# A hybrid decoder layer: 64-row and 64-column products of two heads issued by turns in branches A and C

## The chip, the cores and the metric

The kernel runs on one core of one Trainium2 chip. The time is the device time of one execution in microseconds (us); the median of repeated runs is quoted. All inputs and weights lie in the chip's memory at the start, and all outputs must be written there. One execution was also taken by the hardware profiler, and its records are what this document reads.

## The reference

One inference step of one layer, for a prompt of 1024 tokens and a sample group of 8 x 8 tokens that use the same weights. The model width is 1024. The input projection feeds four token mixers of 256 channels each; their outputs are projected, gated and summed, and attention to a memory and a feed-forward network follow.

```
def _layer(x, ...):
    h = x @ lp['w_in']
    ya = _sb_prompt(q, k, v, bias)      # A: stick-breaking attention, 4 heads x 64
    yb = gb * conv_out                  # B: short gated convolution
    yc, ... = _rwkv7(h[..., OFF_C:OFF_D], ...)   # C: RWKV-7, 4 heads x 64
    yd, sgu_v = _sgu(h[..., OFF_D:], ...)        # D: chunked gating MLP
    gates = sigmoid(x @ w_gate + b_gate)
    x = _ln(ALPHA * x + sum_i(gates_i * (branch_i @ w_branch_i)) @ w_o)
    x = _ln(ALPHA * x + memory attention(x))
    x = _ln(ALPHA * x + (relu(x @ w_up) ** 2) @ w_down)
```

Branch A, for each head and query, sums value rows with weights that are made from the scores of all earlier keys (a sigmoid of the score times the product of the "not stopped" factors after it). Branch C keeps a 64 x 64 state per head:

```
    def step(S, inp):
        r_t, w_t, k_t, v_t, a_t, b_t = inp
        sa = jnp.einsum('nhij,nhj->nhi', S, a_t)
        S = S * w_t[:, :, None, :] + sa[..., None] * b_t[:, :, None, :] + v_t[..., None] * k_t[:, :, None, :]
        return S, jnp.einsum('nhij,nhj->nhi', S, r_t)
```

The prompt begins with a zero state; each of the 8 sample sequences begins with a state of its own, 4 heads each, and its final state is an output.

## The kernel before

All of it is one program on five engines. TensorE (PE) multiplies 128 x 128 weights with up to 512 columns into PSUM; VectorE (DVE), ScalarE (ACT) and GpSimd (POOL) work between PSUM and SBUF, and SyncE (SP) issues most DMAs. A product in plain fp32 leaves two records on PE, one per pass; `mm`, the big projections (L117, L129), is split by hand into high and low parts in a faster type.

In time, the program does branch C at about 105 to 517 us, D to 569, A to 900, then the gates and branch projections, the output projection, the memory attention and the feed-forward network. The branches consist of small products with waits between them. So that PE has work there, `self.fill(step)` at set places draws the next units of the big projections from a generator (`units`): a fixed number of them for each kind of step. Behind that, a scheduler sets the final order on each engine from the code's order and its own estimate of times; the order on each engine is then fixed.

**Branch A** (`branch_a`). A step is one query block `i` of 128 queries, one block `ob` of up to 512 keys, a pair of heads `pr` and a head `hh` of it. The scores `z` (L470) of both heads are multiplied one behind the other; `sb_chunk` (L339 to L354) makes the weights of one head with Exp and Ln on ACT and a running sum on DVE. `turn` transposes them (`wtp`, L497) and copies them to SBUF (`wT`); `values` (L444) then multiplies them with V for that head into its 64 rows of `yps`, up to four products in a row. `late` and `turned` are lists that delay `turn` by two heads and `values` by one more. The sample's own attention (`zp`, L513, and `ysp`, L553) runs between; it already takes two pairs of heads by turns.

**Branch C**, chunks of 256 prompt tokens, in the order 0, sample, 1, 2, 3. `c_blocks` makes for each block of 128 tokens and each pair of heads the transposes `tk` (L947), then for each head four products of 64 rows x 128 columns in the PSUM tile `gr` (L955), which DVE masks into `LM` and `lm` (L956, L957); `c_solve` inverts a triangular matrix: its blocks go to memory (`Ld`) and come back spread out (`Li`, a DMA issued by SP), DVE sets the diagonal of `Li` (a memset, L996), and 31 pairs of DVE operations follow (`tpr`, `Ti`, L1002, L1003). `c_uw` (L1037, L1040) multiplies with the inverse; `c_chain` carries the state S through four steps of 64 tokens per chunk, and in each step multiplies S by WT (L1063), adds on DVE, and updates the state with two products for each pair of heads, tok by tok (L1069) and tok by SA (L1073), each 64 rows to 128 x 128, of which only the two 64 x 64 blocks of the own head are used (L1076). The products of 64 x 64 at L1080 take two heads by turns.

**The sample** (`c_sample`), for each pair of heads: for each head, 8 products `sas` (state times WT, L1105) and 8 products `yss` (state times r, 8 columns, L1106) turn by turn; DVE adds into `SAs` (L1107); a fill; the product `ym` (L1109); then twice a spread tile `ex` by DVE (L1113, 64 x 512) and a product `snp` of 64 rows x 512 columns (L1115). At the pair's end DVE adds `snp` to the state, scales it (L1116, L1117), and adds `yss` and `ym` into Y (L1120).

Of the kernel before, what the change touches and what calls it, by code (L numbers as in the profile page):

```python
# [8 lines left out]
F32 = mybir.dt.float32  # L9
# [20 lines left out]
HR = (slice(0, 64), slice(64, 128))  # L30
# [19 lines left out]
class Kern:  # L50
# [306 lines left out]
    def branch_a(self, ca):  # L357
# [78 lines left out]
        def values(pr, i, ob, hh, w, wT):  # L436

            top = ob == i // 4
            if top and hh == 0:
# [5 lines left out]
            if ob == 0 and hh == 1:  # L445
# [7 lines left out]
        for pr in range(2):  # L453
            smp = self.sample_a(pr, own, bias, am, rows, wP)
            alone = False
            for i in range(8):
# [7 lines left out]
                for ob in range(i // 4, -1, -1):  # L464
# [6 lines left out]
                    for hh in range(2):  # L471
# [10 lines left out]
                        if turned:  # L482
                            values(*turned.pop(0))
# [4 lines left out]
        for a in turned:  # L488
            values(*a)
        for a in late:  # L490
            values(*turn(*a))
# [434 lines left out]
    def c_blocks(self, d):  # L926
# [16 lines left out]
        def products(pr, b):  # L943
# [5 lines left out]
            nc.scalar.copy(X[:nb, pb, :, 1, :], ps[:nb, 0:128].rearrange("p (h i) -> p h i", h=2))  # L949

            lm = cc.tile([128, 2, 2, 128], F32, name="lm", tag="lm", bufs=2)
            for hh in range(2):
                g = self.psw.tile([128, 4, 128], F32, name="gr", tag="gr", bufs=2)
                for j, (p, q) in enumerate(((bh, at), (bh, rt), (kh, at), (kh, rt))):
                    nc.tensor.matmul(g[:nb, j, :nb], p[HR[hh], pr, cs], q[HR[hh], pr, cs], start=True, stop=True)  # L955
                nc.vector.tensor_mul(LM[:nb, pb, hh, :, :nb], g[:nb, 0:2, :nb], lte)  # L956
                nc.vector.tensor_mul(lm[:nb, hh, :, :nb], g[:nb, 2:4, :nb], lte)  # L957
# [86 lines left out]
    def c_chain(self, d):  # L1044
# [3 lines left out]
        wide = lambda pr: slice(128 * pr, 128 * pr + 128)  # L1048
        tok, Mrb, WT, rt, Y, pc = (d[q] for q in ("tok", "Mrb", "WT", "rt", "Y", "pc"))
# [6 lines left out]
        for kx in range(4):  # L1056
# [4 lines left out]
            yps, sn = st[:, 0, 256:384], st[:, 1, 0:256]  # L1061
# [1231 lines left out]
```

## Time and profile before

| what | value |
|---|---|
| median of 3 runs (lowest to highest) | 2307.57 us (2305.55 to 2320.82) |
| the profiled execution's own time | 2307.98 us |
| its span in the trace | 2305.9 us |
| PE matmuls busy | 2213.4 us, 96% |
| weight loads (PEld), beside the matmuls | 1973.8 us, 86% |
| DVE, ACT, POOL busy | 1379.5, 973.6 and 424.9 us |
| chain of waits, PE's share | 74% |

The page sums the busy time of each engine and cuts the span into slices; the table of groups adds the instructions of one line; the timeline gives single instructions or runs of like ones (x8 means eight records from the first's start to the last's end). In the square brackets of a row stand the idle time of its engine before it and what ended that. The ends of matmuls are modelled and they overlap, so from one start to the next is less than a record's duration. PEclk is the granted TensorE clock as a share of full speed: 1.00 is 2.4 GHz, 0.50 is 1.2 GHz.

### The profile page before, as it was taken

What the parts mean: (1) busy time and instruction counts of PE and PEld (TensorE: products, weight loads), DVE (VectorE), ACT (ScalarE), POOL (GpSimd) and SP (SyncE); (2) the same over time, 40 slices, a digit from 0 to 9 for tenths busy, and PEclk for the clock granted to TensorE, in tenths of its full rate; (3) what the DMA queues carried; (4) which work ended last, traced back from release to release, by engine and by line L of the source; (5) the groups of instructions that cost most, each with busy time, mean ns of one, the idle gap of its engine ahead of it and who ended that gap; (6) DMA issues with size and microseconds to landing.
All of it is one profiled execution on the core that took longest, in us unless ns stands there. A gap on an engine that the chain in (4) does not pass through costs nothing.

```text
span 2305.9 us, 36127 instructions
## 1 busy us (share of the span) xinstructions
PE 2213.4 (96%) x13582; PEld 1973.8 (86%) x13582; DVE 1379.5 (60%) x2746; ACT 973.6 (42%) x1880; POOL 424.9 (18%) x484
## 2 busy tenths in 40 slices
PE   8998999999999999999999999999699999999997
PEld 8987687788889989998998878878699999788886
DVE  3357468645666576344333787668576777655548
ACT  4333153125554556444322466425334444543432
POOL 0111111112310310024120410000345454100100
PEclk9999799999999999999999999999899999999999
DMA  5322232135433434555323255633488677975535
GB/s 189 101 75 82 57 107 83 42 106 179 146 130 118 145 97 159 181 164 168 128 71 132 92 197 170 234 108 137 138 286 279 236 238 239 312 255 182 180 122 169
DMA packets 186070, 359.40 MB, mean 156 GB/s; under 512 B 36312, under 2 KB 92776, under 8 KB 185896
## 3 DMA queue, kind: packets, MB, share of 16 engines
q1 hardware_dynamic: 175448, 321.52, 42.7%
q0 software_dynamic: 10448, 35.57, 4.5%
q8 instruction: 107, 1.75, 0.3%
q14 instruction: 67, 0.55, 0.1%
HBM read 252.18 MB, written 104.84 MB: 155 GB/s over the span
## 4 chain that ended last, share of the span: by engine, by line
PE 74%; DMA 9%; DVE 9%; issue 3%; ACT 3%; POOL 1%; SPq 1%; DVEq 0%; ACTq 0%; POOLq 0%
PE mm L117 23%; PE m L117 13%; PE dn L1964 11%; PE mm L129 7%; PE sc L129 3%; PE pp L117 2%; PE yps L444 1%; PE ds L1969 1%; PE wtp L497 1%; PE gr L955 1%; DVE wlo L106 1%; DVE tpr L1002 1%; DMA Li<-Ld 1%; ACT whi L100 1%; DMA add<-gate 1%
## 5 line engine op out<-in xcount | busy, mean ns | idle before, releaser
L117 PE MATMUL mm<-ah,whi 128*128 128x384 f32 (+1 forms) x1176 | 397.1, 338 | 8.4 <-ACT ah L277 4.6
L117 PE MATMUL mm<-al,whi 128*128 128x384 f32 (+1 forms) x1176 | 393.5, 335 | 1.4 <-DVE al L278 1.4
L117 PE MATMUL mm<-ah,wlo 128*128 128x384 f32 (+1 forms) x1176 | 393.6, 335 | 1.1 <-DVE wlo L106 1.1
L1964 PE MATMUL dn<-dop 128*128 128x512 f32 x1344 | 318.8, 391 | 2.9 <-ACT dop L1661 2.7
L1964 PEld LDWEIGHTS dn<-dop 128*128 128x128 f32 x1344 | 251.7, 188 | 60.0 <-ACT dop L1661 4.5
L106 DVE TENSOR_TENSOR wlo<-wraw,whi 128x1024 fp32r<-128x1024 f32 (+2 forms) x177 | 196.2, 1118 | 162.7 <-ACT whi L100 162.3
L100 ACT CAST whi<-wraw 128x1024 fp32r<-128x1024 f32 (+1 forms) x162 | 166.0, 1032 | 257.6 <-PE mm L117 105.3
L117 PEld LDWEIGHTS mm<-ah,whi 128*128 128x128 f32 x1176 | 225.5, 192 | 20.0 <-issue 7.2
L117 PEld LDWEIGHTS mm<-al,whi 128*128 128x128 f32 x1176 | 225.2, 191 | 10.2 <-issue 6.5
L117 PEld LDWEIGHTS mm<-ah,wlo 128*128 128x128 f32 x1176 | 225.5, 192 | 7.0 <-issue 4.4
L1662 DVE TENSOR_TENSOR dop<-wraw,dop 128x512 fp32r<-128x512 f32 x224 | 151.7, 715 | 118.8 <-ACT dop L1661 118.5
L117 PE MATMUL m<-xht,wo 128*128 128x272 f32 x1024 | 202.4, 293 | 18.1 <-ACT wo L1661 10.5
L1661 ACT CAST dop<-wraw 128x512 fp32r<-128x512 f32 x224 | 131.2, 619 | 168.4 <-PE dn L1964 116.2
L117 PEld LDWEIGHTS m<-xht,wo 128*128 128x128 f32 x1024 | 165.5, 192 | 18.9 <-ACT wo L1661 10.7
L129 PE MATMUL mm<-wlo,ah 128*128 128x512 f32 (+1 forms) x488 | 169.1, 349 | 1.5 <-DVE wlo L106 1.4
L129 PE MATMUL mm<-whi,ah 128*128 128x512 f32 (+1 forms) x488 | 169.5, 349 | 0.7 <-ACT stD L636 0.5
L117 PE MATMUL m<-xh,wo 128*128 128x272 f32 x768 | 153.9, 294 | 6.3 <-DVE r L1876 6.3
L129 PE MATMUL mm<-whi,al 128*128 128x512 f32 (+1 forms) x448 | 155.8, 348 | 0.0
L117 PE MATMUL m<-xlt,wo 128*128 128x272 f32 x512 | 149.4, 292 | 0.0
L117 PEld LDWEIGHTS m<-xh,wo 128*128 128x128 f32 x768 | 124.8, 192 | 7.1 <-ACT wo L1661 2.6
L117 PE MATMUL m<-xl,wo 128*128 128x272 f32 x384 | 112.0, 292 | 0.0
L129 PEld LDWEIGHTS mm<-wlo,ah 128*128 128x128 f32 x488 | 92.9, 190 | 15.6 <-DVE wlo L106 2.5
(506 smaller groups left out, 4377.5 us busy)
## 6 DMA issues: line engine op xcount, KB each, us to landing
wraw<-hs SPq DMA_DIRECT2D x112, 256.0 KB, 3.4
wraw<-in_w_up SPq DMA_DIRECT2D x38, 512.0 KB, 4.4
wraw<-in_w_gate SPq DMA_DIRECT2D x32, 512.0 KB, 3.6
dw<-in_w_down SPq DMA_DIRECT2D x32, 512.0 KB, 5.1
hs<-sh SPq DMA_DIRECT2D x64, 256.0 KB, 2.6
wt<-dw SPq DMA_DIRECT2D x32, 512.0 KB, 5.6
wraw<-wt SPq DMA_DIRECT2D x64, 256.0 KB, 4.3
wraw<-in_w_down SPq DMA_DIRECT2D x48, 256.0 KB, 5.5
```

The costliest lines, as they stand in the source:

```text
L100: nc.scalar.copy(hi[:, c], raw[:, c])
L106: nc.vector.tensor_sub(lo[:, c], raw[:, c], hi[:, c].bitcast(F32))
L117: nc.tensor.matmul(ps[:, :n], a, b, start=first and i == 0, stop=last and i == len(steps) - 1, skip_group_check=not first)
L129: nc.tensor.matmul(ps[:, :n], a, b, start=i == 0, stop=i == len(steps) - 1)
L444: nc.tensor.matmul(y["ps"][HR[hh], 0:128], V[pr, ob][:, j, HR[hh]], wT[:, j, :], start=top and j == 0, stop=ob == 0 and j == w // 128 - 1)
L497: self.nc.tensor.transpose(ps[:b.shape[-1], j * 128:j * 128 + 128], b, self.ident)
L955: nc.tensor.matmul(g[:nb, j, :nb], p[HR[hh], pr, cs], q[HR[hh], pr, cs], start=True, stop=True)
L1002: nc.vector.tensor_mul(tv, Ti[:, 0:h, 0:t + 1], Li[:, 0:t + 1, t:t + 1].rearrange("p s o -> p o s").to_broadcast([128, h, t + 1]))
L1661: nc.scalar.copy(o[:, 0], src)
L1662: nc.vector.tensor_sub(o[:, 1], src, o[:, 0].bitcast(F32))
L1964: nc.tensor.matmul(ps[j], hs[:, a, c], w[:, b], start=first and k == 0, stop=last and k == 2, skip_group_check=n >= 16 and steps[n][0] in ...
L1969: nc.tensor.matmul(sp, rows[p][:, smp[i]].rearrange("p a n -> p (a n)"), ops[n][1][:, b], start=i != 2 and p == 0 and b == 0, stop=p == 15 ...
```

## The change

It sets the order of products in four places, and cuts work in two of them.

- **Branch A**: `values` takes both heads of a step. Their products alternate: head 0 into rows 0 to 63 of `yps`, head 1 into rows 64 to 127. `turned` is emptied when it holds two heads, so 24 runs of two heads replace 48 of one.
- **`c_blocks`**: both `gr` tiles are taken at once, and the four products of the two heads alternate.
- **`c_chain`**: the state's update computes only the own head's 64 x 64 block. Per step and term, four products of 64 x 64 replace two of 64 x 128; the alternating heads write different rows of PSUM.
- **`c_sample`**: `sas` of both heads alternate, then `yss` (now in a free part of the tile of `sas`). The two terms of the state's update are laid over one another in 128 rows: `tok` gets a copy in rows 64 to 127 (two more ACT copies per pair), `ex` is filled in both halves, and one product of 128 rows per head replaces two of 64. Three additions into Y replace two. The two fills of a pair stand together behind `yss`.

```diff
-        def values(pr, i, ob, hh, w, wT):
+        def values(*heads):
...
             for j in range(w // 128):
-                nc.tensor.matmul(y["ps"][HR[hh], 0:128], V[pr, ob][:, j, HR[hh]], wT[:, j, :], start=top and j == 0, stop=ob == 0 and j == w // 128 - 1)
+                for *_, hh, _, wT in heads:
+                    nc.tensor.matmul(y["ps"][HR[hh], 0:128], V[pr, ob][:, j, HR[hh]], wT[:, j, :], start=top and j == 0, stop=ob == 0 and j == w // 128 - 1)
...
-                        if turned:
-                            values(*turned.pop(0))
+                        if len(turned) == 2:
+                            values(*turned)
+                            turned.clear()
...
+            if smp:
+                nc.scalar.copy(tok[64:128, pb, 0, :], ps[0:64, 256:384])
+                nc.scalar.copy(tok[64:128, pb, 2, :], ps[0:64, 384:512])
...
+            g = [self.psw.tile([128, 4, 128], F32, name="gr", tag="gr", bufs=2) for _ in range(2)]
+            for j, (p, q) in enumerate(((bh, at), (bh, rt), (kh, at), (kh, rt))):
+                for hh in range(2):
+                    nc.tensor.matmul(g[hh][:nb, j, :nb], p[HR[hh], pr, cs], q[HR[hh], pr, cs], start=True, stop=True)
...
-            for pr in range(2):
-                nc.tensor.matmul(sn[:, wide(pr)], tok[q, 2 * pr + b, 1], tok[q, 2 * pr + b, 2], start=pr == 0, stop=False)
+            for pr, hh in own:
+                nc.tensor.matmul(sn[HR[hh], cols(pr)], tok[q, 2 * pr + b, 1, HR[hh]], tok[q, 2 * pr + b, 2, HR[hh]], start=pr == 0, stop=False)
...
-            for pr in range(2):
-                nc.tensor.matmul(sn[:, wide(pr)], tok[q, 2 * pr + b, 0], flat(SA[q, pr]), start=False, stop=pr == 1)
+            for pr, hh in own:
+                nc.tensor.matmul(sn[HR[hh], cols(pr)], tok[q, 2 * pr + b, 0, HR[hh]], SA[q, pr, hh, :], start=False, stop=pr == 1)
...
+            for hh, R in enumerate(HR):
+                spread(HR[1], tok[64:128, 2 * pr, 2, R], hh)
+            for s in range(8):
+                for hh, R in enumerate(HR):
+                    nc.tensor.matmul(st[0:64, hh, 0:64], wx[R, 64 * s:64 * s + 64], S0[R, s, :], start=s == 0, stop=s == 7, skip_group_check=True)
...
+            for s in range(8):
+                for hh, R in enumerate(HR):
+                    nc.tensor.matmul(st[R, hh, 64 + 8 * s:72 + 8 * s], S0[R, s, :], rt[R, pr, 8 * s:8 * s + 8], start=hh == 1 and s == 0, stop=s == 7, skip_group_check=True)
+            self.fill("smp")
+            self.fill("smp")
...
+            for hh, R in enumerate(HR):
+                spread(HR[0], SA[0:64, R], hh)
+            for hh, R in enumerate(HR):
+                nc.tensor.matmul(snp[R], tok[:, 2 * pr, 0, R], ex[hh], start=True, stop=True)
```

`spread` is the DVE multiplication that fills one half of an `ex` tile.

In branch A on PE (`yps<-wT,v` is a product of the weights of one head with V, and the number behind wT tells the heads apart), one head's run before:

```order
L444 MATMUL yps_5649<-wT_5652,v_5285 64x128 [waits DVE_49]
L444 MATMUL yps_5649<-wT_5652,v_5285 64x128
L497 MATMUL wtp_5742<-ident_75,z_5596 128x128 [waits PE_49,Activation_49]
L497 MATMUL wtp_5742<-ident_75,z_5596 128x128
L497 MATMUL wtp_5742<-ident_75,z_5596 128x128 [waits Pool_49]
```

And the two heads' run now, at the same step:

```order
L446 MATMUL yps_5795<-wT_5616,v_5345 64x128
L446 MATMUL yps_5795<-wT_5709,v_5345 64x128 [waits DVE_49]
L446 MATMUL yps_5795<-wT_5616,v_5345 64x128
L446 MATMUL yps_5795<-wT_5709,v_5345 64x128
L502 MATMUL wtp_5802<-ident_75,z_5656 128x128 [waits PE_49,Activation_49]
```

The two products of the other head (wT_5556), which stood in a run of their own some 55 rows earlier, have moved between those of the second.

On PE in branch C's chunk 1, the first half of one block's `gr` products before (gr_2270 is head 0's tile, gr_2277 head 1's):

```order
L117 MATMUL mm_2559<-ah1_82,wlo_2195 128x384
L955 MATMUL gr_2270<-at_2113,bh_2114 128x128 [waits DVE_49]
L955 MATMUL gr_2270<-rt_2117,bh_2114 128x128
L955 MATMUL gr_2277<-at_2113,bh_2114 128x128
L955 MATMUL gr_2277<-rt_2117,bh_2114 128x128
L117 MATMUL mm_2559<-ah1_82,whi_2194 128x384
```

And now:

```order
L117 MATMUL mm_2575<-al1_85,whi_2214 128x384
L965 MATMUL gr_2290<-at_2133,bh_2134 128x128 [waits DVE_49]
L965 MATMUL gr_2291<-at_2133,bh_2134 128x128
L965 MATMUL gr_2290<-rt_2137,bh_2134 128x128
L965 MATMUL gr_2291<-rt_2137,bh_2134 128x128
L117 MATMUL mm_2575<-ah1_82,wlo_2215 128x384
```

Two products of a head in a row have become one and one. In other blocks the scheduler keeps four products of one head and then four of the other, since the second tile is not free sooner; of the 18 products of two heads, each of eight multiplications, about five come out by turns that were not before.

On DVE in the sample's first pair of heads before (SAs is the sum, ex the spread tile, Li and tpr belong to `c_solve` of chunk 1):

```order
L1113 TENSOR_TENSOR ex_2532<-tok_1591,cmask_880 64x512
L996 MEMSET Li_2394 128x32 [waits DMAHW3_49]
L1002 TENSOR_TENSOR tpr_2396<-Ti_2395,Li_2394 128x2 [waits DMAHW2_49,DVE_49]
L1003 TENSOR_REDUCE Ti_2395<-tpr_2396 128x1 [waits DMAHW5_49,DVE_49]
L1002 TENSOR_TENSOR tpr_2396<-Ti_2395,Li_2394 128x3 [waits DVE_49]
L1003 TENSOR_REDUCE Ti_2395<-tpr_2396 128x1 [waits DVE_49]
L1002 TENSOR_TENSOR tpr_2396<-Ti_2395,Li_2394 128x4 [waits DVE_49]
L1003 TENSOR_REDUCE Ti_2395<-tpr_2396 128x1 [waits DVE_49]
L1002 TENSOR_TENSOR tpr_2396<-Ti_2395,Li_2394 128x10 [waits DVE_49]
L1107 TENSOR_TENSOR SAs_2483<-sas_2481,X_1592 64x64 [waits PE_49]
L1003 TENSOR_REDUCE Ti_2395<-tpr_2396 128x2 [waits DVE_49]
L1113 TENSOR_TENSOR ex_2586<-SAs_2483,cmask_880 64x512 [waits DVE_49]
```

And now:

```order
L1128 TENSOR_TENSOR SAs_2502<-sas_2500,X_1592 64x64 [waits PE_49]
L1128 TENSOR_TENSOR SAs_2502<-sas_2500,X_1592 64x64
L1118 TENSOR_TENSOR ex_2503<-SAs_2502,cmask_880 64x512 [waits DVE_49]
L1007 MEMSET Li_2414 128x32 [waits DMAHW4_49]
L1118 TENSOR_TENSOR ex_2504<-SAs_2502,cmask_880 64x512 [waits DVE_49]
L1013 TENSOR_TENSOR tpr_2416<-Ti_2415,Li_2414 128x2 [waits DMAHW2_49,DVE_49]
```

The memset of Li, which waits for a DMA, has moved from ahead of the second head's SAs to ahead of the second head's ex.

## Rows read from the trace of the kernel before

**Rows 1.** Busy time of each engine, its share of the span and instructions (the page's first part).

```profile
PE 2213.4 (96%) x13582; PEld 1973.8 (86%) x13582; DVE 1379.5 (60%) x2746; ACT 973.6 (42%) x1880; POOL 424.9 (18%) x484
```

**Rows 2.** Windows: busy us (count) of PE, PEld, DVE, ACT, POOL; clock, DMA share, GB/s.

```profile
250.90:291.90 41.00, 39.64 (x207) 24.72 (x203) 16.95 (x66) 3.44 (x8) 1.14 (x2) 0.58 0.15 45
291.90:517.00 225.10, 216.44 (x1442) 181.58 (x1442) 149.74 (x403) 71.66 (x156) 31.34 (x54) 0.98 0.27 82
569.00:900.00 331.00, 325.47 (x2261) 297.69 (x2261) 207.42 (x389) 180.70 (x357) 61.05 (x78) 0.99 0.42 134
```

**Rows 3.** PE groups by shape: busy us, mean ns, idle before and its releaser.

```profile
L444 PE MATMUL yps<-wT,v 128*64 128x128 f32 x288 | 41.6, 281 | 0.0
L1115 PE MATMUL snp<-ex,tok 64*64 64x512 f32 x16 | 15.2, 1078 | 0.0
L1069 PE MATMUL st<-tok 64*128 64x128 f32 x64 | 11.3, 297 | 1.5 <-DVE Ti L1003 1.5
L955 PE MATMUL gr<-at,bh 64*64 64x64 f32 x8 | 1.0, 239 | 3.6 <-DVE bh L882 2.7 <-DVE lm L957 0.9
```

**Rows 4.** PE timeline in branch A: start us, duration us, then the instruction.

```profile
633.96 0.34 PE L117 MATMUL mm<-al,whi 128*128 128x384 f32 x1
634.14 0.34 PE L117 MATMUL mm<-ah,wlo 128*128 128x384 f32 x1
634.41 1.09 PE L444 MATMUL yps<-wT,v 128*64 128x128 f32 x8
635.42 0.33 PE L497 MATMUL wtp<-ident,z 128*128 128x128 f32 x1
```

**Rows 5.** PE timeline: the sample's scores in branch A, two pairs by turns.

```profile
624.90 1.07 PE L513 MATMUL zp<-kp,qb 128*32 128x128 f32 x16
```

**Rows 6.** PE timeline in branch C: products of 64 x 64 and of 64 x 128.

```profile
204.65 0.45 PE L1080 MATMUL st<-LM,SA 64*64 64x64 f32 x8
207.94 0.71 PE L1069 MATMUL st<-tok 64*128 64x128 f32 x4
```

**Rows 7.** PE timeline: two blocks' gr products in branch C.

```profile
224.33 0.50 PE L955 MATMUL gr<-at,bh 64*128 64x128 f32 x4
224.66 0.40 PE L955 MATMUL gr<-rt,bh 64*128 64x128 f32 x4
224.98 0.44 PE L117 MATMUL mm<-ah,whi 128*128 128x384 f32 x1
...
241.05 0.48 PE L955 MATMUL gr<-at,bh 64*128 64x128 f32 x2
...
242.69 0.42 PE L117 MATMUL mm<-ah,wlo 128*128 128x320 f32 x1
```

**Rows 8.** Windows of the sample's stretch, columns as in rows 2.

```profile
250.90:254.30 3.40, 3.40 (x61) 3.12 (x57) 0.98 (x5) 0.37 (x2) 0.00 (x0) 1.00 0.53 133
254.30:271.40 17.10, 15.74 (x49) 8.76 (x45) 6.81 (x31) 0.48 (x1) 0.59 (x1) 0.50 0.12 43
...
274.80:291.90 17.10, 17.10 (x53) 9.88 (x53) 8.44 (x27) 2.59 (x5) 0.54 (x1) 0.50 0.10 31
```

**Rows 9.** The same stretch, the projections' line L117 alone.

```profile
250.90:291.90 41.00, 17.57 (x49) 13.53 (x50) 0.58 0.15 45
```

**Rows 10.** DVE timeline in the sample: start us, duration us, the instruction, idle before.

```profile
254.40 0.68 DVE L1113 TENSOR_TENSOR ex<-tok,cmask 64x512 f32<-64x512 f32 x1
259.32 0.09 DVE L996 MEMSET Li<- 128x32 f32 x1 [4.24 <-DMA Li<-Ld]
...
260.70 0.21 DVE L1107 TENSOR_TENSOR SAs<-sas,X 64x64 f32<-64x64 f32 x1
```

**Rows 11.** PE timeline in the sample: the product behind the second head's SAs.

```profile
260.96 0.47 PE L1109 MATMUL ym<-LM,SAs 64*64 64x64 f32 x2 [1.36 <-DVE SAs L1107]
```

**Rows 12.** Loads of ACT's function tables at L354: ns min/median/max, start us.

```profile
L354 ACT ACT_TABLE_LOAD  x1: 1283/1283/1283, 883.4 to 883.4; - x1
```

More of the change, by code (lines that the diff above doesn't have):

```diff
@@ L434, in turn @@
             return pr, i, ob, hh, w, wT
-        def values(pr, i, ob, hh, w, wT):
+        def values(*heads):
+            pr, i, ob, _, w, _ = heads[0]
             top = ob == i // 4
-            if top and hh == 0:
+            if top:
                 y["ps"] = self.wk_ps("yps", "y")
@@ L443, in values @@
             for j in range(w // 128):
-                nc.tensor.matmul(y["ps"][HR[hh], 0:128], V[pr, ob][:, j, HR[hh]], wT[:, j, :], start=top and j == 0, stop=ob == 0 and j == w // 128 - 1)
-            if ob == 0 and hh == 1:
+                for *_, hh, _, wT in heads:
+                    nc.tensor.matmul(y["ps"][HR[hh], 0:128], V[pr, ob][:, j, HR[hh]], wT[:, j, :], start=top and j == 0, stop=ob == 0 and j == w // 128 - 1)
+            if ob == 0:
                 nc.vector.tensor_copy(y["T"][:, i % 4 * 128:i % 4 * 128 + 128], y["ps"][:, 0:128])
@@ L487, in branch_a @@
                 self.fill("z")
-        for a in turned:
-            values(*a)
         for a in late:
-            values(*turn(*a))
+            if len(turned) == 2:
+                values(*turned)
+                turned.clear()
+            turned.append(turn(*a))
+        values(*turned)
     def transpose_sb(self, blocks):
@@ L1048, in c_chain @@
         wide = lambda pr: slice(128 * pr, 128 * pr + 128)
+        own = [(pr, hh) for pr in range(2) for hh in range(2)]
         tok, Mrb, WT, rt, Y, pc = (d[q] for q in ("tok", "Mrb", "WT", "rt", "Y", "pc"))
@@ L1060, in c_chain @@
             st = self.psa.tile([128, 2, 512], F32, name="st", tag="st")
-            yps, sn = st[:, 0, 256:384], st[:, 1, 0:256]
+            yps, sn = st[:, 0, 256:384], st[:, 1, 0:128]
             for pr in range(2):
@@ L1097, in c_sample @@
             nc.vector.tensor_copy(wx[:, 504:512], WT[:, pr, 56:64])
-            yps, ym = self.wk_ps("yss"), self.wk_ps("ym")
+            ym = self.wk_ps("ym")
             st = self.psa.tile([128, 2, 512], F32, name="sas", tag="st")
@@ L1101, in c_sample @@
             SA = cc.tile([128, 128], F32, name="SAs", tag="SA", bufs=2)
-            for hh in range(2):
-                R = HR[hh]
-                for s in range(8):
-                    nc.tensor.matmul(st[0:64, hh, 0:64], wx[R, 64 * s:64 * s + 64], S0[R, s, :], start=s == 0, stop=s == 7)
-                    nc.tensor.matmul(yps[R, 8 * s:8 * s + 8], S0[R, s, :], rt[R, pr, 8 * s:8 * s + 8], start=s == 0, stop=s == 7)
-                nc.vector.tensor_add(SA[0:64, R], st[0:64, hh, 0:64], X[0:64, 2 * pr, hh, 0, :])
-                self.fill("smp")
-                nc.tensor.matmul(ym[R, 0:64], SA[0:64, R], Mrb[0:64, 2 * pr, hh, 0:64], start=True, stop=True)
-                for i, (src, lh) in enumerate(((SA[0:64, R], tok[0:64, 2 * pr, 0, R]), (tok[0:64, 2 * pr, 2, R], tok[0:64, 2 * pr, 1, R]))):
-                    ex = self.ct("ex").rearrange("p r n -> p (r n)")[0:64, 0:512]
-                    nc.vector.tensor_mul(ex.rearrange("p (s e) -> p s e", e=64), src[:, None, :].to_broadcast([64, 8, 64]),
-                                         cm[0:64, 640:648, None].to_broadcast([64, 8, 64]))
-                    nc.tensor.matmul(snp[R], lh, ex, start=i == 0, stop=i == 1)
+            ex = [self.ct("ex").rearrange("p r n -> p (r n)")[:, 0:512] for _ in range(2)]
@@ L1116, in c_sample @@
+            for hh, R in enumerate(HR):
+                spread(HR[0], SA[0:64, R], hh)
+            for hh, R in enumerate(HR):
+                nc.tensor.matmul(snp[R], tok[:, 2 * pr, 0, R], ex[hh], start=True, stop=True)
             nc.vector.tensor_add(S0, S0, snp.rearrange("p (s i) -> p s i", i=64))
@@ L1118, in c_sample @@
             nc.gpsimd.dma_start(O["s_wkv"][pr], S0.rearrange("p s i -> p (s i)"))
-            for p in (yps, ym):
-                nc.vector.tensor_add(Y[:, pr, 0:64], Y[:, pr, 0:64], p[:, 0:64])
+            for hh, R in enumerate(HR):
+                nc.vector.tensor_add(Y[R, pr, 0:64], Y[R, pr, 0:64], st[R, hh, 64:128])
+            nc.vector.tensor_add(Y[:, pr, 0:64], Y[:, pr, 0:64], ym[:, 0:64])
     def c_norm(self, d):
```

14 lines of the change are left out of this document (7 added, 7 removed).

## The prediction

> **What bounds the kernel now.** First the sums of busy time: PE 2213.4 us of a span of 2305.9, 96%, while DVE has 60% and ACT 42% [rows 1]. Then the same by stage, in windows, since the change touches three stages only: in branch A PE is busy for 325.47 of 331.00 us, DVE for 207.42 and ACT for 180.70; in the last chunks of branch C 216.44 of 225.10; in the sample's stretch 39.64 of 41.00 [rows 2]. So in each stage PE is what time is made of, and a product that goes away, or goes beside another, gives its time back, because a unit of the big projections stands behind it in PE's queue. What PE does not do now is little (5.5 us in A, 1.4 in the sample). Last the granted clock: 0.99 in A and 0.98 in C's last chunks, but 0.58 in the sample's stretch [rows 2], and there it is cut in pieces: 1.00 for 3.40 us, 0.50 (1.2 GHz) for 17.10 us, and once more the same; both low pieces begin where runs of 64-row products (`sas`, `yss`) have just ended and `snp` begins [rows 8].
>
> The sum is made against the profiled execution, 2307.98 us, which lies 0.41 above the median of the runs, 2307.57. About 1% (23 us) is what a measurement of this kernel can tell from no change, so faster means below 2284.5 and slower above 2330.6.
>
> **Branch A, `values`.** 288 records of `yps` are 41.6 us of busy PE [rows 3], in 48 runs. A run of eight lasts 1.01 us from its start to the next instruction's, 126 ns a record, and is entered 0.27 us after the start of the last `mm`, where two `mm` follow one another in 0.18 [rows 4]. What two products by turns cost is in the same branch: the sample's `zp`, 16 records, writes 32 columns of each of two pairs by turns and lasts 1.07 us, as long as the eight of `yps` (1.09) [rows 4, 5]. So two heads in turn should take the time of one: 41.6 / 2 = −20.8 us. That 24 runs are entered and not 48 would give another 24 x (0.27 − 0.18) = 2.2 us; I keep that for the lower bound, −23.0. The waits: no record of `yps` waited for anything [rows 3], and `turned` is emptied before the next head is appended, so the second head's `wT` has had one step to be copied, as before; the order shows a wait for DVE at the second head's first product, which I take to be long over. Price of one that isn't: 24 runs, and behind it stand `wtp` and `z`, on which ACT waits.
>
> There is a side effect at A's end. The order of ACT has 36 loads of function tables instead of 32: with the steps bundled otherwise, the gate's sigmoids now lie between the last Exp and Ln of branch A. One load is 1.283 us [rows 12]; four are 5.1 us. Before `wtp` of the last steps PE waits for that chain, and the fillers there are few. Bounds 0 and 5.1; I take +3, since the last head's chain meets most of them. Branch A: −18, from −23 to −16.
>
> **Branch C, `c_blocks`.** In the order before, one half block is A, A, B, B (two products of each head). In the trace the four `at` records start together and the four `rt` follow, and all eight take 0.65 us (224.33 to 224.98); a whole block in the order AAAABBBB takes 1.64 us for 16 (241.05 to 242.69) [rows 7]. So where the order was AABB, nothing is won by turning, and where it was AAAABBBB, 1.64 − 2 x 0.65 = 0.34 us per block. There are 18 blocks in all (16 of the prompt, 2 of the sample), −6.1 if all turned, but the order changes about five of them: −1.7.
>
> Here two rules of the Trainium skill pull in opposite ways. "TensorE: Matmul & The Clock Gate", section "Part 3: Packing small matmuls — row/col tiling", says that matmuls start and end strictly in program order. By it, A, A, B, B could not overlap A with B and turning would win at every half block, some 18 x 0.34 more or −6 in all; this trace does not agree, with its 0.65 us for eight records out of program order. "TensorEngine Tiling (Array Packing)", section "PSUM Bottleneck", says that packing makes the products faster but not the reading out of PSUM, which can become the limit.
>
> That limit has its place in this change: both `gr` tiles are taken at once, so a block's first product waits for both masks of the block before on DVE, with `mm` behind it in PE's queue. The nearest row of such a wait is `gr` of the sample, 3.6 us behind DVE, 0.9 of it for the mask `lm` [rows 3]. If each of 18 blocks waited 0.4 us, about half of that, it is +7; in most blocks the fill lies between, and I take +0.7. `c_blocks`: −1, from −6 to +7.
>
> **Branch C, `c_chain`.** Per step two terms, each four records of 64 x 128, become eight of 64 x 64 with two heads by turns. Four of the old kind last 0.71 us; L1080 is the new kind exactly, the same rows and the same alternating columns, and eight last 0.45 [rows 6]. The gain is 0.26 for each term. L1069 has 64 records, so 16 steps [rows 3], and L1073, the other term, the same: 32 x −0.26 = −8.3. If the heads did not run side by side, eight records of half the columns would be no gain, and one entry more (0.27 − 0.18) for each term would make it 32 x 0.09 = +3. I take −8: DVE's reading of `sn` is the same in number and size.
>
> **The sample.** Before, 41.0 us, of which 49 records of `mm` take 17.57 [rows 9]; elsewhere they would take 49 x 0.18 = 8.8 [rows 4], so the sample itself costs 32.2. After:
> - `sas` and `yss`: the same 128 records, by turns as wholes; as before 2 x 3.4 = 6.8 [rows 8].
> - `snp`: 16 records become 8, of 128 rows. Each now takes 15.2 / 16 = 0.95 us at the low clock [rows 3, 8]. In the first pair the heads come one after the other (next point), 4 x 0.95 = 3.8; in the second side by side, 1.9. Sum 5.7.
> - A new wait. DVE's memset of `Li` waited 4.24 us for its DMA, until 259.32, and the second head's SAs and `ym` stood behind it (`ym` waited 1.36) [rows 10, 11]. Now it stands ahead of the second head's `ex`, on which that head's `snp` waits, and behind that all of PE's queue. `Li` lands 8.4 us after the stretch begins (250.9), `ex` takes 0.68, so that `snp` can start at 9.1. PE is there at 3.4 + 0.7 (SAs) + 0.7 (`ex`) + 1.9 (head 0's `snp`) = 6.7: it waits 2.4. I take 3, as PE may get there sooner.
> - `mm`: only 12 records stand in the stretch now, and some ten behind it may still run at the low clock, each 0.36 instead of 0.18 [rows 4, 9]: 22 x 0.18 = 4.0. The other fills run later at 0.18.
> - The four copies on ACT go beside PE's transposes and products: 0.
>
> Sum 6.8 + 5.7 + 3 + 4.0 = 19.5, with 0.7 for `ym` 20.2: 32.2 − 20.2 = −12. Bounds: if the clock stays at 1.00 and nothing waits, 6.8 + 2.9 + 1 = 10.7, a gain of 21.5; if it falls twice for 17.10 us as now, half of which is lost (8.55 each), and the wait is 4.8, then 10.7 + 4.8 + 17.1 − 2.4 (a low clock costs nothing while PE waits) = 30.2, a gain of 2.
>
> **Sum.** −18 − 1 − 8 − 12 = −39: 2307.98 − 39 = 2269.
>
> **The rivals.**
> 1. *The sample's clock stays up.* With a third of the `snp` work gone and PE waiting in between, the low pieces may not come at all. Then the sample gives −18 to −21: about 2262. For it: the falls follow a dense run of 64-row products. Against: `sas` and `yss` are denser now than before.
> 2. *The sample gives nothing.* Both low pieces come, the `Li` wait is on PE, and A's end pays all four table loads: −2 instead of −12 and +2: 2281. For it: the 17.10 us pieces came after both pairs alike.
> 3. *A is paced by another engine.* If the chain of a head's weights through ACT and DVE sets when `wtp` can go, half of A's 21 us turns into waits of PE: 2269 + 10.5, about 2280. For it: little, at 180.70 and 207.42 of 331 us busy [rows 2].
> 4. *The halved products don't run side by side*, and the chain gives +3 instead of −8: 2280. Against it stands L1080 itself.
> 5. *Slower.* The granted clock falls in branch A and the chain as it does in the sample, because they now run the same kind of paired 64-wide products. Each low piece of 17.10 us loses 8.55; 39 / 8.55 = 4.6 of them cancel the gain, 62 / 8.55 = 7.3 make the kernel slower by 1%; with 8 it is 2269 + 68 = 2337. For it: rows 8. Against: A already has paired `zp` and `ysp` and 48 runs of `yps` at a clock of 0.99, and the last chunks of C their paired L1080 at 0.98 [rows 2].
>
> That the change doesn't do what it says holds for `c_blocks`, where the order keeps most blocks unturned; the forecast has that in it.
>
> **How the numbers follow.** The forecast 0.55 (its own range 2262 to 2277), rival 1 0.17, rival 2 0.12, rival 3 0.08, rival 4 0.05, rival 5 0.03. The range is 2252 to 2286: below, the bounds of A and of the sample together (another 5 and 9.5, with 2 of `c_blocks`); above, rivals 2 to 4 with the waits at `gr`. Faster by over 1% takes the forecast, rival 1 and most of 2 to 4: 0.87. Within 1%: two of rivals 2 to 4 together, or few low pieces of rival 5, 0.11. Slower by over 1%: 0.02.
>
> **What would show it.** In the changed trace the `yps` records should be busy near 21 us in about 24 runs; the two update terms of a chain step should last 0.45 each; the sample's stretch, to the next chunk's work, about 25 us with a wait for DVE before the second `snp` of the first pair of 2 to 5 us; low-clock pieces are read from the windows there; and at A's end up to 3 us of PE before `wtp`, released by ACT, with table loads beside it. The prediction is wrong if `yps` by turns stays near 41 us, if A's window shrinks by less than 12 us, or if the clock in A or in the chain falls below 0.95.

## The result, and the profile after

| | before | changed |
|---|---|---|
| median (lowest to highest) | 2314.20 us (2305.55 to 2321.45, 4 runs) | 2278.07 us (2273.76 to 2281.47, 4 runs) |
| ratio, 95% interval | 1 | 0.9837, 0.9809 to 0.9866 |
| profiled execution | 2307.98 us | 2281.47 us |

The kernel became 1.6% faster: 2307.57 x 0.9837 = 2270 us against a forecast of 2269. (The medians are 36 us apart, and 2278.07 is 9 us above 2269: the forecast starts from an execution of 2307.98, which is quicker than the kernel before usually is, 2314.20 in these four runs.) The sum was right; two of its four terms were not, and they missed in opposite directions. The first sums of the page after (compare [rows 1]):

```profile
span 2279.7 us, 36377 instructions
...
PE 2175.1 (95%) x13702; PEld 1949.2 (86%) x13702; DVE 1374.5 (60%) x2748; ACT 978.7 (43%) x1888; POOL 425.7 (19%) x484
```

PE is busy for 38.3 us less, but the span is only 26.2 us shorter in these two executions: waits grew by some 12 us. The mean granted clock is nearly the same in both, 0.978 and 0.977, so the low clock that the sample loses (below) stands elsewhere in this one execution. The groups of PE by shape in the changed kernel (compare [rows 3]):

```profile
L502 PE MATMUL wtp<-ident,z 128*128 128x128 f32 x152 | 27.8, 294 | 5.8 <-ACT z L354 5.8
L446 PE MATMUL yps<-wT,v 128*64 128x128 f32 x288 | 22.5, 282 | 0.0
L1085 PE MATMUL st<-SA,tok 64*64 64x64 f32 x128 | 7.9, 248 | 0.0
L1081 PE MATMUL st<-tok 64*64 64x64 f32 x128 | 7.9, 248 | 0.5 <-DVE SA L1076 0.5
L558 PE MATMUL ysp<-vp,wP 128*32 128x128 f32 x128 | 8.8, 281 | 5.4 <-DMA vp<-in_vpages,pt 5.4
L1139 PE MATMUL snp<-ex,tok 128*64 128x512 f32 x8 | 4.1, 734 | 2.6 <-DVE ex L1118 2.6
```

And the two groups of the kernel before whose waits grew, in the same view:

```profile
L497 PE MATMUL wtp<-ident,z 128*128 128x128 f32 x152 | 27.5, 291 | 0.5 <-ACT z L354 0.5
L553 PE MATMUL ysp<-vp,wP 128*32 128x128 f32 x128 | 8.5, 276 | 2.3 <-DMA vp<-in_vpages,pt 2.3
```

The third column is where the reader finds what A gave back: `wtp` waits 5.8 us for ACT instead of 0.5, and the sample's value products 5.4 us for a DMA instead of 2.3. In the second column `yps` has gone from 41.6 to 22.5, the two update terms of the chain from 22.6 to 15.8, and `snp` from 15.2 to 4.1. That is more than the half that the cut gives: six of the eight records run at the full clock, and in the second pair the two heads run side by side, as the rows below show. Windows of the sample's stretch, and of a stretch of the chain (PE, PEld, DVE, ACT, POOL, clock, DMA share, GB/s; compare [rows 8]):

```profile
253.30:258.70 5.40, 4.41 (x75) 2.98 (x74) 1.24 (x5) 0.13 (x2) 0.00 (x0) 1.00 0.33 110
258.70:265.50 6.80, 5.18 (x37) 3.02 (x38) 3.73 (x18) 2.21 (x3) 0.59 (x1) 0.50 0.02 5
265.50:269.00 3.50, 3.50 (x45) 2.00 (x44) 2.25 (x10) 2.18 (x3) 0.00 (x0) 1.00 0.55 153
330.40:350.90 20.50, 20.50 (x108) 16.55 (x109) 11.57 (x45) 4.30 (x9) 2.26 (x5) 0.50 0.00 1
```

The sample's own products now run from 253.3 to 269.0, 15.7 us, of which 6.8 at 1.2 GHz, where they had 34.2 of 41.0. But a piece of 20.5 us at 1.2 GHz stands in the chain of a prompt chunk, where the kernel before had one of 3.4 us. Over the whole stretch behind the sample, 269.0 to 494.2 us, the clock is 0.95; [rows 2] has 0.98 there. Inside the sample, PE's timeline (start, duration, instruction, idle before; compare [rows 11]) and DVE's (compare [rows 10]):

```profile
253.32 1.15 PE L1126 MATMUL sas<-S,wx 64*64 64x64 f32 x32
...
256.64 1.07 PE L1139 MATMUL snp<-ex,tok 128*64 128x512 f32 x2
260.32 1.97 PE L1139 MATMUL snp<-ex,tok 128*64 128x512 f32 x2 [2.62 <-DVE ex L1118]
...
268.00 1.08 PE L1139 MATMUL snp<-ex,tok 128*64 128x512 f32 x4
```

```profile
254.79 0.68 DVE L1118 TENSOR_TENSOR ex<-SAs,cmask 64x512 f32<-64x512 f32 x1
259.62 0.65 DVE L1118 TENSOR_TENSOR ex<-SAs,cmask 64x512 f32<-64x512 f32 x1 [4.16 <-issue]
259.64 0.09 DVE L1007 MEMSET Li<- 128x32 f32 x1
```

The new wait is where it was forecast: the second head's `ex` starts only when the memset has been released, and PE stands 2.62 us (3 had been taken). The second pair shows what side by side is worth: four records in 1.08 us, as long as the two records of one head at the same clock (256.64).

At branch A's end, ACT and the PE transpose that waits for it:

```profile
847.33 1.28 ACT L1310 ACT_TABLE_LOAD   x1
848.62 0.61 ACT L1310 ACTIVATE add<-add,vec 128x384 f32<-128x384 f32 x1
849.26 1.28 ACT L347 ACT_TABLE_LOAD   x1
850.55 0.72 ACT L347 ACTIVATE e<-e,eps 128x512 f32<-128x512 f32 x1
...
858.37 1.28 ACT L354 ACT_TABLE_LOAD   x1
859.67 1.15 ACT L354 ACTIVATE z<-z 128x512 f32<-128x512 f32 x2
```

```profile
860.35 1.12 PE L502 MATMUL wtp<-ident,z 128*128 128x128 f32 x4 [3.98 <-ACT z L354]
```

Six loads of 1.28 us lie between 847.33 and 859.67, among the last two heads' Ln and Exp (two in the kernel before, the second the one of [rows 12]), and PE waits 3.98 us behind them (3 had been taken).

### The profile page after: what moved, and what is told of

Its sections match the earlier page's. It is cut to its first block, busy times and chain, and to the rows that moved or that the text cites. A ratio compares the mean times of both kernels' runs of the same rounds, so it can differ in the third digit from the quotient of the medians.

```text
span 2279.7 us, 36377 instructions
## 1 busy us (share of the span) xinstructions
PE 2175.1 (95%) x13702; PEld 1949.2 (86%) x13702; DVE 1374.5 (60%) x2748; ACT 978.7 (43%) x1888; POOL 425.7 (19%) x484
## 4 chain that ended last, share of the span: by engine, by line
PE 71%; DVE 10%; DMA 9%; issue 4%; ACT 3%; POOL 2%; SPq 1%; DVEq 0%; ACTq 0%; POOLq 0%
PE mm L117 21%; PE m L117 12%; PE dn L1989 11%; PE mm L129 8%; PE sc L129 3%; PE pp L117 3%; PE ds L1994 1%; DVE tpr L1013 1%; DVE wlo L106 1%; DMA vp<-in_vpages,pt 1%; ACT whi L100 1%; DMA Li<-Ld 1%; PE wtp L502 1%; DVE Ti L1014 1%; PE gr L965 1%
## 5 line engine op out<-in xcount | busy, mean ns | idle before, releaser
L117 PE MATMUL mm<-ah,whi 128*128 128x384 f32 (+1 forms) x1176 | 395.7, 336 | 8.4 <-ACT ah L277 4.9
L117 PE MATMUL mm<-al,whi 128*128 128x384 f32 (+1 forms) x1176 | 392.5, 334 | 0.6 <-DVE al L278 0.6
L117 PE MATMUL mm<-ah,wlo 128*128 128x384 f32 (+1 forms) x1176 | 391.7, 333 | 0.6 <-DVE wlo L106 0.6
L117 PEld LDWEIGHTS mm<-ah,whi 128*128 128x128 f32 x1176 | 224.4, 191 | 18.0 <-ACT ah L277 5.5
L117 PEld LDWEIGHTS mm<-al,whi 128*128 128x128 f32 x1176 | 224.1, 191 | 7.0 <-issue 3.5
L117 PEld LDWEIGHTS mm<-ah,wlo 128*128 128x128 f32 x1176 | 224.1, 191 | 4.3 <-issue 1.9
L117 PE MATMUL m<-xht,wo 128*128 128x272 f32 x1024 | 202.7, 293 | 16.8 <-ACT wo L1686 10.5
L117 PEld LDWEIGHTS m<-xht,wo 128*128 128x128 f32 x1024 | 165.8, 192 | 17.7 <-ACT wo L1686 10.7
L117 PE MATMUL m<-xh,wo 128*128 128x272 f32 x768 | 153.6, 293 | 6.1 <-DVE r L1901 6.1
L117 PE MATMUL m<-xlt,wo 128*128 128x272 f32 x512 | 149.5, 292 | 0.0
L117 PEld LDWEIGHTS m<-xh,wo 128*128 128x128 f32 x768 | 124.7, 192 | 6.7 <-ACT wo L1686 2.6
L117 PE MATMUL m<-xl,wo 128*128 128x272 f32 x384 | 111.9, 292 | 0.0
```

Of the source, the lines that this page charges most:

```text
L117: nc.tensor.matmul(ps[:, :n], a, b, start=first and i == 0, stop=last and i == len(steps) - 1, skip_group_check=not first)
```

## The experiments

**Theory.** Each part acts on its own stage, and PE's time goes straight into the span; branch A gives back some 8 us in waits that the new order and the shorter products bring, and the sample gains more than forecast because the low clock goes with its long 64-row products. **Rivals**: the waits in A are chance and it is worth 18; the clock in the sample is chance; the paired 64-wide products pull the clock down elsewhere; the wait for both masks makes `c_blocks` slower. Ratios are to the kernel before on the same chip, with 95% intervals.

### One part at a time

`a_alone` is the kernel before with the diff of `values`, `turned` and `late`; `sample_alone` with that of `c_sample`, the two `tok` copies and the mask; `chain_alone` with that of `c_chain`; `gr_alone` with the two `gr` tiles and the turned loops. The edits are the pieces of the diff above; of `c_chain`'s, for example:

```diff
+            for pr, hh in own:
+                nc.tensor.matmul(sn[HR[hh], cols(pr)], tok[q, 2 * pr + b, 1, HR[hh]], tok[q, 2 * pr + b, 2, HR[hh]], start=pr == 0, stop=False)
```

> The kernel before with branch A's turned value products alone. Theory 1 (the products halve, but the end of the branch gives part back): the product records of values take 20 to 21 us of TensorE's time instead of 38, TensorE's idle time in branch A rises by 6 to 9 us (about 4 of it before one transpose at the branch's end with four more table loads on ScalarE, the rest before the sample's value products, which wait for a DMA), and the kernel is 6 to 12 us faster. Rival (the idle time was chance): idle time as before, 17 to 20 us faster.

> The kernel before with the sample's part alone (both terms laid over one another, products by turns, two more copies). Theory 1 (the short low-clock stretch comes from this part): the low-clock time between the sample's first products and its last falls from 34 us to 7 to 10, a wait of 2 to 4 us for VectorE stands before the second state product of the first pair, and the kernel is 17 to 20 us faster. Rival (the clock there was chance): 10 to 13 us faster, with a low stretch of 17 us.

> The kernel before with the chain's own-head blocks alone. Theory 1: the two update terms take 0.38 us of TensorE's time per step and term instead of 0.64, 8 us faster in all, and the granted clock in the chain stays as before. Rival (paired 64-wide products pull the clock down): a low-clock stretch of about 20 us appears in the chain of a prompt chunk, 10 us are lost, and the kernel is as fast as before.

> The kernel before with the block products of two heads by turns alone. Theory 1 (two heads in blocks of two already overlap): their records take 2 to 4 us less of TensorE's time and idle time before them rises by 1 to 2 us: 0 to 3 us faster, which is the same within what can be measured. Rival (a wait for both masks): 2 to 7 us slower.

| part | forecast, us | ratio (95%) | of 2315.29 us |
|---|---|---|---|
| branch A | −18 | 0.9952 (0.9936 to 0.9968) | −11 |
| sample | −12 | 0.9923 (0.9898 to 0.9948) | −18 |
| chain | −8 | 0.9972 (0.9956 to 0.9987) | −6.5 |
| `gr` | −1 | 0.9999 (0.9982 to 1.0017) | 0 |
| sum | −39 | 0.9846 | −36 |

The parts add up: 1.54% against the 1.63% of the whole. **A**: theory 1 (the records take 22.5 us, from 41.6). The three groups in `a_alone`, with the same waits as in the whole:

```profile
L502 PE MATMUL wtp<-ident,z 128*128 128x128 f32 x152 | 27.9, 295 | 6.1 <-ACT z L354 6.0
L446 PE MATMUL yps<-wT,v 128*64 128x128 f32 x288 | 22.5, 282 | 0.0
...
L558 PE MATMUL ysp<-vp,wP 128*32 128x128 f32 x128 | 8.5, 276 | 4.7 <-DMA vp<-in_vpages,pt 4.7
```

Busy 41.6 to 22.5 is −19.1; the waits grow by 5.6 at `wtp` and 2.4 at `ysp`; −19.1 + 8.0 = −11.1, which is what the ratio of the runs gives. The two profiled executions themselves differ by 4.7 us only (spans of 2305.9 and 2301.2), since their mean clocks differ (0.978 and 0.974): the sample of `a_alone`, for one, has 40.9 us of low clock instead of 34.2.

**Sample**: theory 1. Its window at the low clock:

```profile
262.50:269.30 6.80, 5.76 (x39) 3.40 (x39) 4.31 (x20) 2.21 (x3) 0.59 (x1) 0.50 0.08 5
```

One profile could be chance, but every execution's mean clock is on record. It averages 0.976 in the kernel before (25 executions) and 0.980 in `sample_alone` (6); `a_alone`, `chain_alone` and `gr_alone` have 0.975, 0.976 and 0.975. At half clock, half of the time is lost, so (1 − clock) x span estimates the loss: 57 us before and 46 in `sample_alone`. By this estimate some 10 of the 18 us are the clock's, and of the four parts only the sample's raises it.

**Chain**: theory 1 in size, 7.4 + 7.7 us for the two terms where [rows 3] gives 11.3 for one; in the sample's stretch its clock is that of the kernel before, 34.2 us low. Later in the chain its profile has 17.1 us of low clock where the kernel before has 6.8, so the rival may have something in it, but not the 10 us it asked for; `gr_alone`, whose chain is the one before, has 13.6 us of low clock there too.

**`gr`**: theory 1. The records take less (12.6 us for `at`,`bh` instead of 13.6 and so on), the idle time before them fell from 5.7 to 3.1 us where a rise of 1 to 2 was expected, and nothing of it is seen in the time. Its interval is 4 us to either side, so a gain of up to 4 us isn't excluded. In this execution the sample's two low pieces have run together into one, with the sample's code as before:

```profile
260.30:301.20 40.90, 38.45 (x151) 23.71 (x151) 16.13 (x62) 2.73 (x5) 1.14 (x2) 0.50 0.10 31
```

### The sample's two halves

In `stack_only` the terms are laid over one another, and the heads stay in their order:

```diff
-                for i, (src, lh) in enumerate(((SA[0:64, R], tok[0:64, 2 * pr, 0, R]), (tok[0:64, 2 * pr, 2, R], tok[0:64, 2 * pr, 1, R]))):
-                    ex = self.ct("ex").rearrange("p r n -> p (r n)")[0:64, 0:512]
...
+                for P, src in ((HR[1], tok[64:128, 2 * pr, 2, R]), (HR[0], SA[0:64, R])):
...
+                nc.tensor.matmul(snp[R], tok[:, 2 * pr, 0, R], ex, start=True, stop=True)
```

In `turns_only` the new order stands, with two products of 64 rows per head:

```diff
+            for i in range(2):
+                for hh, R in enumerate(HR):
+                    src, lh = ((SA[0:64, R], tok[0:64, 2 * pr, 0, R]), (tok[0:64, 2 * pr, 2, R], tok[0:64, 2 * pr, 1, R]))[i]
...
+                    nc.tensor.matmul(snp[R], lh, ex, start=i == 0, stop=i == 1)
```

> The kernel before with one half of the sample's part: both terms of the state's update over one another in 128 rows (one product per head instead of two, the two copies), while the heads and the products sas and yss stay in their old order. Theory 1 (the half of the long 64-row products that goes is what kept the clock low): low-clock time in the sample falls from 34 us to under 15, and the kernel is 10 to 15 us faster. Rival (the clock hangs on sas and yss and on the heads one after the other): low-clock time stays near 34, 4 to 8 us faster.

> The kernel before with the other half of the sample's part: sas, then yss of both heads by turns, both fills behind them, but two products of 64 rows per head for the state's update, the heads by turns where their tiles allow. Theory 1: low-clock time in the sample stays above 25 us, 3 to 8 us faster. Rival (turns are what ends the low clock): under 15 us of low clock, 10 to 15 us faster.

Both came to the same: 0.9948 (0.9929 to 0.9967) and 0.9947 (0.9930 to 0.9965), 12 us each, where together they give 18. So did `snp`, in the groups of PE, first `stack_only`:

```profile
L1118 PE MATMUL snp<-ex,tok 128*64 128x512 f32 x8 | 5.9, 825 | 0.0
```

then `turns_only`:

```profile
L1121 PE MATMUL snp<-ex,tok 64*64 64x512 f32 x16 | 5.9, 732 | 3.6 <-DVE ex L1119 3.6
```

And so did the low clock, one window of each:

```profile
261.40:271.60 10.20, 10.20 (x64) 6.60 (x62) 3.59 (x17) 0.51 (x1) 0.00 (x0) 0.50 0.08 22
```

```profile
261.70:271.90 10.20, 7.63 (x34) 5.19 (x36) 5.94 (x29) 0.48 (x1) 0.59 (x1) 0.50 0.16 53
```

Theory 1 holds for the stacking, and fails for the turns: there the rival was right. `snp` goes from 15.2 to 5.9 us of PE time in either way (part of that is the clock's own doing), and with it two thirds of the sample's low clock (34.2 to 10.2 us), so neither the number of products nor their rows is what it hangs on alone. The mean clocks agree: 0.979 (7 executions) and 0.980 (10) against 0.975 (22), by the estimate above some 9 and 10 of the 12 us. What exactly starts and ends the low clock isn't settled by this. In its profiled execution `turns_only` also has the longest low piece of all behind the sample, though its chain is the one before:

```profile
312.90:340.20 27.30, 27.30 (x124) 21.94 (x125) 7.05 (x23) 6.67 (x23) 3.07 (x2) 0.50 0.23 61
```

### Mending what the change gave back

`no_table_loads` keeps the gates' sigmoids out of branch A, by a bias that is copied behind the last Exp; `a_mended` is `a_alone` with the same edit.

```diff
+                        if pr == 1 and i == 7 and ob == 0 and hh == 1:
+                            nc.gpsimd.tensor_copy(self.gv[:, 0:1], wt[:, 0:1])
+                            nc.gpsimd.tensor_copy(self.gv, self.vec[:, 0:32])
...
-                nc.scalar.activation(sg, src, AF.Sigmoid, bias=self.vec[:, 8 * i + m:8 * i + m + 1])
+                nc.scalar.activation(sg, src, AF.Sigmoid, bias=(self.gv if early else self.vec)[:, 8 * i + m:8 * i + m + 1])
```

> The changed kernel, in which the early gates' sigmoids take their bias from a copy that GpSimd makes behind the last Exp of branch A, so that none of them lies between that branch's Exp and Ln. Theory 1 (four more loads of function tables are the wait at the branch's end): the wait of 4 us before one transpose there is gone, 30 loads instead of 36, and the time is 3 to 5 us below the changed kernel's (ratio to before near 0.982). Rival (the last heads' chain is late anyway): the wait stays within 1 us and the time is that of the changed kernel.

> The kernel before with branch A's turned products, and with the early gates' sigmoids behind the last Exp of the branch. Theory 1 (half of what branch A lost is the table loads): 3 to 5 us below branch A's products alone, ratio to before 0.993 to 0.994; the wait of 4 us before one transpose is gone. Rival: the ratio of branch A's products alone, 0.995.

There are 30 loads instead of 36, and of the wait of 3.98 us 0.90 is left, now for another engine: the loads were its cause. The same transpose in `no_table_loads`:

```profile
854.44 0.63 PE L506 MATMUL wtp<-ident,z 128*128 128x128 f32 x4 [0.90 <-DVE wT L434]
```

The time does not follow as surely: 0.9824 (0.9799 to 0.9849) beside the changed kernel's 0.9837, but 0.9967 (0.9951 to 0.9982) beside `a_alone`'s 0.9952. The first can't be put down to the mend: the five executions of `no_table_loads` have a mean clock of 0.984, those of `after_again` (the changed kernel on the same chip) 0.979, which by the estimate above is some 11 us, more than the difference of their medians (2277.41 and 2279.82). In the profiles, the stretch from the first `z` to the last `yps` is 302.2 us in `a_mended` against 307.9 in `a_alone`, and the stretch behind it, to the first transpose after the gates, 405.5 against 398.8. Part of that is a fill that moved across the border (16 `mm` records, 2.8 us), and part a new wait of 1.7 us among the gates, whose sigmoids now come later; the remaining 2 us are not traced to a cause. For the time of the whole, the rival's number stands.

`ex_on_pool` moves the second head's `ex` to GpSimd, out of the memset's way:

```diff
-                spread(HR[0], SA[0:64, R], hh)
+                spread(HR[0], SA[0:64, R], hh, nc.gpsimd if hh else nc.vector)
```

> The changed kernel with the second head's spread tile of the sample computed by GpSimd instead of VectorE, so that it no longer stands behind the memset that waits for a DMA. Theory 1 (that memset is the wait): the wait of 2.6 us before the second state product of the first pair goes to under 1 us, both heads' products then run side by side, and the time is 2 to 5 us below the changed kernel's. Rival (GpSimd is slower at it, or the next wait takes its place): a wait of 1.5 us or more remains in the sample and the time is within 2 us of the changed kernel's.

```profile
256.97 1.08 PE L1139 MATMUL snp<-ex,tok 128*64 128x512 f32 x4
261.52 1.97 PE L1126 MATMUL sas<-S,wx 64*64 64x64 f32 x32 [3.47 <-issue]
```

The first pair's `snp` now run side by side at the full clock, and PE waits all the same, 3.47 us, one place on: the second pair's `sas` needs the one PSUM tile that the first pair's additions into Y on DVE still read, and they stand behind the same memset. Ratio 0.9858 (0.9836 to 0.9881): the rival. What holds PE there is the DMA of `Li`, which lands when it lands; only work that needs neither `Li` nor that tile would cover it. And the clock has its part: behind these products it is low for 17.1 us, where the changed kernel had 6.8, and the second pair's `snp` run at half clock:

```profile
258.90:276.00 17.10, 14.48 (x95) 10.39 (x96) 11.30 (x46) 8.14 (x13) 3.01 (x5) 0.50 0.16 53
```

`both_mends` has both edits:

> The changed kernel with both mends, the gates' bias behind the last Exp and the second head's spread tile on GpSimd. Theory 1: the two gains add, 5 to 9 us below the changed kernel, ratio to before 0.979 to 0.981. Rival: the granted clock takes the gain back in branch C, no more than 3 us below the changed kernel.

Ratio 0.9830 (0.9804 to 0.9856), 2 us below the changed kernel: the rival's number, but not its reason, since the mean clock is higher here (0.983). Its profiled execution is the quickest of all profiled (2272.21 us), and its clock says why: one low piece of 13.6 us that begins in the sample and one of 3.4 after it in the chains.

```profile
260.80:274.40 13.60, 13.04 (x65) 8.99 (x66) 10.21 (x38) 6.71 (x12) 3.01 (x5) 0.50 0.18 59
342.70:346.10 3.40, 3.36 (x15) 2.81 (x17) 3.15 (x9) 1.19 (x3) 0.25 (x1) 0.50 0.00 0
```

### The changed kernel without `gr`, and once more

```diff
-            g = [self.psw.tile([128, 4, 128], F32, name="gr", tag="gr", bufs=2) for _ in range(2)]
...
+            for hh in range(2):
+                g = self.psw.tile([128, 4, 128], F32, name="gr", tag="gr", bufs=2)
```

> The changed kernel with the block products of branch C as before, one head after the other. Theory 1: within 2 us of the changed kernel's time (ratio to before 0.983 to 0.985), since the turned products alone gave nothing. Rival (they matter once the sample and the chain are shorter): 3 us or more slower than the changed kernel.

0.9843 (0.9819 to 0.9868), as theory 1 had it: the turned `gr` products are worth nothing that can be measured here either.

> The changed kernel as it is, on the chip of this group. Theory 1 (its two levels of time, 2274 and 2281, come from low-clock stretches in the chains of branch C that are there in some executions only): ratio to before 0.982 to 0.986, and the low-clock time between 300 and 420 us differs from the first profile's 20.5 us by 7 us or more wherever the time differs by 4 us or more. Rival: the same low stretch in the same place.

`after_again` has no edit. Ratio 0.9847 (0.9824 to 0.9871), as the first time. The profiled execution took 2276.86 us, 4.6 less than the first one's 2281.47. Low windows of it in the sample and behind it:

```profile
257.20:264.00 6.80, 5.20 (x37) 3.03 (x38) 3.75 (x18) 2.21 (x3) 0.59 (x1) 0.50 0.03 4
328.90:335.70 6.80, 6.80 (x46) 6.00 (x45) 3.79 (x17) 0.39 (x2) 0.80 (x2) 0.50 0.01 2
339.10:345.90 6.80, 6.80 (x42) 6.22 (x42) 5.09 (x17) 2.52 (x4) 1.48 (x3) 0.50 0.00 0
363.00:366.40 3.40, 3.27 (x12) 2.98 (x13) 3.40 (x9) 0.47 (x2) 0.00 (x0) 0.50 0.21 22
```

6.8 + 6.8 + 3.4 = 17.0 us instead of 20.5: less than the 7 us of difference that theory 1 named, so it fails as stated. Of low clock ahead of the sample the first execution had 20.5 and this one 13.7; with that, branch C's low clock differs by some 10 us, of which half, 5 us, is time lost, against a difference of 4.6. Between these two executions the time so follows the low pieces of the whole branch, not that one. The five new times (2275.30 to 2284.95 us) don't fall on two levels; of all nine, the quickest, 2273.76, has a mean clock of 0.981 and the slowest, 2284.95, of 0.976.

## Why the prediction was right

- **PE's time is the span's**: right in the main. The parts add up to the whole, and no other engine took over a stage; but of 38.3 us that PE has less to do, some 12 came back as waits in the profiled pair.
- **A, −18, measured −11**: wrong. The halving was forecast at −20.8 and is −19.1. The table loads' wait was forecast at 3 and is 3.98, of which 0.90 stays when the loads go. The step that failed was the one on the waits, "no record of `yps` waited for anything": it asked only what the moved products wait for, and not what else in the branch was on time because those products took so long. Two waits it left out: the other waits of `wtp` for ACT (1.8 to 2.0 us, 0.5 before; in none of the kernels without the turned products more than 0.8) and the wait for the sample's `vp` (+3.1 in the changed kernel, +2.4 in `a_alone`). The second is less sure: over all profiles it is 2.8 to 5.6 us with the turned products and 2.0 to 3.6 without. `vp` has one buffer: its gather is issued when PE has read the one before, and PE now comes back for it with less work between; that this is the cause is argued, as a second buffer was not tried.
- **`c_blocks`, −1, measured 0** (−4 to +4): right, for the reason given: A, A, B, B already overlapped, which [rows 7] show. They stand against the strict program order that the Trainium skill's "TensorE: Matmul & The Clock Gate" states in "Part 3: Packing small matmuls — row/col tiling". `gr_alone` agrees, but decides less, as most blocks stayed unturned. The wait at PSUM's reading, of which the Trainium skill's "TensorEngine Tiling (Array Packing)" warns in "PSUM Bottleneck", hardly grew at `gr`: the sample's `gr` waits 1.1 us for a mask after, 0.9 (of 3.6 in all) before. The prompt's `gr` of `at` and `bh` wait more in the changed kernel, 4.5 us instead of 0.9, but 4.4 of that for the operand `bh`, not for a mask.
- **Chain, −8, measured −6.5** (−3 to −10): right, taken from a row of the same kind of product; PE's busy time for the two terms fell by 7.5 us, 22.6 to 15.1.
- **Sample, −12, measured −18**: the mechanism was right and the size was off. The new wait was 2.62 us for 3. Mis-sized were three terms, read here from one start to the next. `snp` was 5.7 and is 4.0, and the low clock's cost at the `mm` records was 4.0 and is 1.7, because the clock came back before the end; `sas`, `yss` and `ym` were 7.5, from windows of the kernel before, and are 5.4. With 11 `mm` records in the 15.7 us, the sample costs 15.7 − 11 x 0.18 = 13.7 instead of 32.2: a gain of 18.5, near the 18 of the runs. Rival 1, a clock that stays up, with −18 to −21, was the better forecast in number, though 6.8 us of low clock did come. (Its "third of the `snp` work" is a half: 16 records became 8.)
- **Rival 3** came in size, in A alone: 8 us of waits for its 10.5, two thirds of them at `wtp` for ACT as it said (most of that the table loads), a third for a DMA, which it did not name.
- **Rivals 2, 4 and 5** did not come. Of rival 5 there may be a trace: 20.5 us of low clock in the chain, and between 312 and 500 us 14 to 24 us in five of the six profiles with the sample's and the chain's part (3.4 in `both_mends`) against 6.8 before, some 5 us of loss. But its reason, the chain's own paired products, isn't shown: `turns_only` has 30.7 us and `gr_alone` 13.6 there with the chain as it was.
- **Its signs of being wrong**: one came. Branch A's stretch, from the first `z` to the end of the last `yps`, went from 313.8 to 310.2 us (308.2 in `a_alone`), less than the 12 us that were asked for. Besides the waits, 17 `mm` records (some 3 us) moved into it, and its clock was 0.98 instead of 0.99. The clock in the chain, 0.95 in the changed kernel's first profile, stands about at the bound that was set.

Two misses of 7 and 6 us in opposite directions made a total that was off by little. That the total came out so near is luck; the terms of the chain and of `c_blocks` are not.

## What to carry to other kernels

When work leaves the engine that sets the pace, list the waits that were nearly there: every load or chain that was just in time because that engine was slow, and how long it takes from its own release. Products that already run in blocks of two per head overlap across the blocks; interleaving them further was worth nothing that could be measured here (ratio 0.9999), while single-head runs between other work nearly halved when two heads alternated (`yps`, 41.6 to 22.5 us). And where a stretch runs at half clock, a cut in its dense products can bring back the clock of all that runs there: here 34.2 us of low clock became 10.2, whichever way the cut was made. Look then for low clock in other stretches, and compare the mean clock over many executions before a difference of a few us is put down to an edit.

## What the runs showed of the hardware

- Low pieces of clock behind the sample's products: 34.2 us in two pieces in the kernel before and in `chain_alone`, 40.9 in one in `gr_alone` and in `a_alone` (254.6 to 295.5), whose sample is the same code; 10.2 with either half of the sample's change. With both it was 6.8 in four profiles, 3.4 in `no_table_loads`, and 17.1 and 13.6 in the two kernels with one `ex` on GpSimd. The same program had different low pieces in two executions.
- Two products of 64 columns from different heads, each in its own 64 rows of PSUM, take as long as one: 1.08 us for four records of 128 rows x 512 columns, 1.07 for two.
